# A two-layer decoder trunk on one core: first weights on ScalarE's queue, the norms' vectors in front of x, the first products in another order, and a planner with new durations and a margin for TensorE

## The chip, the core and the metric

One NeuronCore of a Trainium2 chip. The metric is the device time of one launch in microseconds (us), the median of several runs. Engines: PE (TensorE; PEld is its weight load), DVE (VectorE), ACT (ScalarE), POOL (GpSimd), SP (SyncE, which here issues nearly all DMAs).

## What is computed

A trunk of two layers over 256 tokens with 1024 features, in float32; layer 0 mixes by block attention, layer 1 by a three-branch sparse attention, and each is followed by a gated per-layer embedding.

```python
for i in range(2):
    h = rms_norm(x, norm_gain[i])
    x = x + (moba_layer if i == 0 else nsa_layer)(h, ...)
    gate = sigmoid(rms_norm(x, ple_gate_gain[i]) @ ple_w_gate[i])
    x = x + gate * (p[i] @ ple_w_proj[i])
def moba_layer(h):
    q, k, v, z = split(h @ w_in, 4)          # 1024 columns each
    return (attention(rope(norm(q)), rope(norm(k)), v) * silu(z)) @ w_out
```

With 256 tokens and blocks of 256 the first layer is plain causal attention over 16 heads.

## The kernel before

All of x (features on partitions, 8 k-tiles of 128 by 256 tokens) stays on the core; the weights, 59 MB in all, stream through. A product is made from three: every operand is split into a rounded part `hi` and a remainder `lo` (for x: `ah` and `al`), and PE forms hi·ah, hi·al and lo·ah. `hi` and `ah` are made on ACT (some on DVE), `lo` and `al` on DVE: `lo` = raw - hi. A weight tile is two k-tiles of 512 columns (128x1024, 512 KB), with five buffers each for `raw`, `hi` and `lo`. The norm's scale comes in late: products are made from x times its gain, and 1/rms is applied to their results, so PE can start before the norm is known.

The program is recorded, not issued: `Plan.record` notes each operation with what it reads and writes and its cost in ns (`Plan.cost`), `Plan.schedule` simulates the engines in order of time and gives each engine its order, and `Plan.emit` issues it. So every instruction has the one line L366 (`emit`), and whatever changes a cost changes the order on all engines. The choice in `schedule`: for each engine the ready operation with the smallest (earliest start, recorded number), then the engine whose choice starts first.

The start: PE runs 15 products of zeros (`warm`). Meanwhile SP issues x's first k-tile, half of the first weight tile, x's second k-tile, the second weight tile, and so on; ACT's queue issues the norms' vectors (`gain_in`, 16 KB) and the other half of the first weights, loads its function table with a tiny Exp (`early`), and makes `ah`. The first unit `uq0` (512 columns of q) takes one k-tile at a time, k = 0 to 7, into banks of PSUM `mm`; then `norm` sums the squares (`sqacc`) over partitions by PE products with `ones` (written to `tr`), DVE makes `ms` from it, and the unit `uk` (k of the first half of the heads) follows with tiles of 128x1024, which need `lo` from DVE. `tq` and `tk` are DVE products of the rotary tables `cst` with the heads' gains `gmoba`, two SP transfers. Then come v, the attention of 8 heads in pairs (`sm` are its probabilities, transposed by PE into `tr`; `hl`, `qk` the split q and k; `s` the scores), the second half, the gate z, the output product, the embedding, and the second layer in the order of `ORDER`, where `kg`, `pc`, `kcB`, `vcB` belong to its branches.

Of the kernel before, what the change touches and what calls it, by code (L numbers as in the profile page):

```python
# [7 lines left out]
F32 = mybir.dt.float32  # L8
# [11 lines left out]
SWITCH, POW = 150.0, 2300.0  # L20
NRAW, NHI, NLO, NPT, NA = 5, 5, 5, 9, 9
WARM = 15
ORDER = ("vw KE vs VS KT QE0 0A 0S1 0S0 VW 0T0 0S3 0T1 kc 0S2 1A 0T3 0T2 KC 1S0 1T0 q1.0 1S2 W0 q1.1 q1.2 1S3 "
         "0V 1T2 q1.3 W1 1S1 W2 1T3 W3 QE1 2A WE 2S2 0c 2S0 1c 1T1 1V 2T0 0b 2T2 2c 2S1 1b 2B 3A 3c 2T1 2S3 "
         "3S1 2T3 2V 3S0 3T1 3T0 3B 3S3 3S2 3T2 3T3 3V")
# [57 lines left out]
class Plan:  # L83
# [77 lines left out]
    def cost(self, op, views, first):  # L161
        n = first.elems() if isinstance(first, View) else 0
        e, m = op.engine, op.method
        if e == "sync":
            v = first if isinstance(first, View) else op.args[1]
            return v.elems() * 4 * v.ap.ap[0][1]
        if e == "tensor":
            k, c = op.args[1].ap.ap[0][1], op.args[1].ap.ap[1][1]
            op.mode = tuple(128 if x > 64 else 64 if x > 32 else 32 for x in (k, c))
            if m == "transpose":  # L170
                return 109.2
            if op.args[1].ap.dtype == mybir.dt.bfloat16:
                return 2.5 + n / 1.2
            if op.args[1].ap.dtype == F32R:
                return (n + 32) / 2.4 if n > 128 else 110

            return 2 * max(54.6 if op.mode == (128, 64) else 109.2, 2 * n / 2.4 / (2 if op.mode == (128, 64) else 1))
        if e == "gpsimd":
            if op.kwargs.get("op") == OP.pow:
                return POW + 130.0 * n  # L180
            return 100 + 2.3 * n
        psum = any(self.tags[v.tile.tag]["psum"] for v in views)
        rows = first.ap.ap[0][1]
        half = 110 if rows in (60, 64) and (any(v.box()[0] != first.box()[0] for v in views)
                                            or psum and first.ap.dtype == F32R and e == "vector") else 0
        if e == "scalar":
            if m == "dma_start":
                return first.elems() * 4 * first.ap.ap[0][1]
            if first.tile.tag == "early":
                return 1500.0  # L190
            c = (60 if psum else 100) + 0.833 * max(n, op.args[1].elems())
            return half + c + 93 * sum(isinstance(op.kwargs.get(k), View) for k in ("scale", "bias", "accum_out"))
        if m == "tensor_tensor_reduce":
            return 130 + 1.04 * n
        if m == "reciprocal":
            return 65 + 6.9 * n
        if m == "tensor_reduce":
            return 65 + 1.04 * op.args[1].elems()
        two = len([v for v in views if v.elems() > 2 and v is not first]) > 1
        if not psum and not two and m in ("tensor_copy", "tensor_scalar"):  # L200
            return 70 + half + 0.52 * n + 60 * any(isinstance(x, View) and x.elems() == 1 for x in op.args[2:])
        if m == "tensor_tensor" and args_step(op.args[1]) >= 16:
            return 65 + 1.75 * n
        return 65 + half + 1.04 * n + (65 if m == "scalar_tensor_tensor" and isinstance(op.args[2], View) else 0)

    LAT = {"PE": 200.0, "DVE": 140.0, "ACT": 160.0, "POOL": 200.0, "DMA": 100.0}
    START = {"PE": 110.0}

    ISSUE, LAG, RATE = 450.0, 2250.0, ((6000.0, 225.0), (26000.0, 280.0), (1e9, 340.0))
    OWN = {"DVE": 127.0, "POOL": 127.0}  # L210

    def lat(self, a, b):
# [24 lines left out]
    def schedule(self):  # L237
# [43 lines left out]
        while len(order) < n:  # L281
            best = None
            for e, lst in ready.items():
                if not lst:
                    continue
                if e in forced:
                    lst = [forced[e]]
                f = free[e]
                ch = None
                for i in lst:  # L290
                    at = alloc_time(i)
                    if at is None:
# [10 lines left out]
                if ch and (best is None or ch < best[0]):  # L303
                    best = (ch, e)
            if best is None:
                raise RuntimeError("no order")
            (s, i), e = best
            o = ops[i]
            for w in o.ways:
                ready[self.ENGINES[w[0]]].remove(i)  # L310
# [77 lines left out]
def trunk(ctx: ExitStack, tc: tile.TileContext, a, out):  # L388
# [44 lines left out]
    cosc, sinc = cs("cosc")[:60], cs("sinc")[:60]  # L433
    repl = cs("repl")[:60].rearrange("p (g r) -> p g r", g=4)

    neg_half = consts.tile([P, 16], F32, name="neg_half")
    nc.vector.memset(neg_half, -0.5)
    warm = work.tile([P, T], mybir.dt.bfloat16, tag="sm", name="warm", bufs=5)
    nc.vector.memset(warm, 0.0)
    ones = consts.tile([P, 2], F32, name="ones")  # L440
    nc.vector.memset(ones, 1.0)

# [8 lines left out]
    def load(src, n, small=False, queue=None):  # L451
        raw = tmp("raw") if small else wpool.tile([P, 1024], F32, tag="raw", name="raw", bufs=NRAW)
        raw = raw[:, :n]
        (queue or nc.sync).dma_start(raw, src)
        return raw
# [13 lines left out]
    def split_act(src, gain=None):  # L469
        hi = apool.tile([P, T], F32R, tag="ah", name="ah")  # L470
        lo = apool.tile([P, T], F32R, tag="al", name="al")
        if gain is None:
            nc.scalar.activation(hi, src, AF.Copy)
            nc.vector.tensor_tensor(lo, src, hi.bitcast(F32), op=OP.subtract)
        else:
            nc.scalar.activation(hi, src, AF.Copy, scale=gain)
            nc.vector.scalar_tensor_tensor(lo, src, gain, hi.bitcast(F32), op0=OP.mult, op1=OP.subtract)
        return hi, lo

    class Unit:  # L480
# [14 lines left out]
        def mul(self, w, j, k, b, ms=(0, 1), cols=None):  # L495
            (wh, wl), (xh, xl) = w, self.xs[k]
            first, last = k == 0, k == self.nk - 1
            if self.feat:
# [7 lines left out]
            else:  # L506
                c0, c1 = cols or (0, self.n)
                o, s = self.ps[b][:, c0:c1], slice(b * P, b * P + P)
                nc.tensor.matmul(o, xh[:, s], wh[:, j], start=first and c0 == 0, stop=False, skip_group_check=True)
                nc.tensor.matmul(o, xl[:, s], wh[:, j], start=False, stop=False, skip_group_check=True)  # L510
                nc.tensor.matmul(o, xh[:, s], wl[:, j], start=False, stop=last, skip_group_check=True)

        def step(self, g):
            w = self.weights(g)
# [218 lines left out]
    uq0.ps = [bank("mm", 4) for _ in range(2)]  # L733

    since = len(nc.ops)
    second = load(a["moba_in"][0, 0, :, 256:512], 256, True, nc.scalar)
    nc.scalar.activation(consts.tile([P, 16], F32, name="early"), neg_half, AF.Exp)
    nc.together(since)
    for k in range(KT):
        nc.sync.dma_start(xT[:, k], a["x"][:, k])  # L740
        x0.append(split_act(xT[:, k], ng[:, 0, k:k + 1]))
        n = 256 if k == 0 else 512
        for c in range(0, 512, n):
            c0 = 512 * (k % 2) + c
            w = split(a["moba_in"][0, k // 2, :, c0:c0 + n], (1, n), small=k < 4, raw=second if c else None)
            for b in range(2):
                uq0.mul(w, 0, k, b, cols=(c, c + n))
    tab, held_at = [], []

    def moba_half(h):  # L750
# [475 lines left out]
def _arrays(i):  # L1226
    import numpy as np

    def c(v):
        return np.ascontiguousarray(v)  # L1230

    def feat(v):
        return c(v.reshape(KT, P, T).transpose(1, 0, 2))
# [11 lines left out]

    f32 = np.float32
    r = {}
    r["x"] = feat(i["x"][0].T)
    r["p"] = c(i["p"][:, 0].transpose(0, 2, 1).reshape(2, 2, P, T).transpose(2, 0, 1, 3))
    r["gain_in"] = c(np.concatenate([gains(i["norm_gain"]), gains(i["ple_gate_gain"])], 1))  # L1250
# [74 lines left out]
```

## Time and profile before

| what | value |
|---|---|
| three runs | 370.11, 370.19, 370.64 us; median 370.19 us |
| the profiled execution's own time | 370.02 us |
| its span (first to last instruction of the program) | 368.2 us |
| busy share of the span: PE, PEld, DVE, ACT | 98%, 88%, 88%, 73% |
| chain that ended last | PE 77%, DVE 13%, ACT 3%, time of issue 3% |
| granted TensorE clock | full from 3.9 us on |

Matmuls are pipelined, so a busy PE is no sign that it is at its peak: PE's pace is read from the starts of successive products, and its idle time from what the product or its weight load waited for. Time is lost where a product starts late, not where an engine off the chain rests.

### The profile page before, as it was taken

The numbers are of one execution on the slowest core, as the hardware profiler recorded it, in microseconds if no ns is written. First come the engines' busy times: TensorE is split into PE (matmuls) and PEld (weight loads), VectorE is DVE, ScalarE is ACT, GpSimd is POOL, SyncE is SP. The second block draws the span as 40 slices with busy tenths as digits, with TensorE's granted clock in tenths as the row PEclk, the third lists the DMA queues.
The fourth block names the chain that finished last, engine by engine and source line by source line (L and its number), as shares of the span: only waits on it lengthen the run. The fifth ranks groups of instructions, "written<-read, shape, count | busy, mean of one in ns | idle before, by whom it ended". The sixth has DMA issues, their size and how long they took to land.

```text
span 368.2 us, 7137 instructions
## 1 busy us (share of the span) xinstructions
PE 359.8 (98%) x2576; PEld 323.2 (88%) x2576; DVE 325.5 (88%) x803; ACT 268.1 (73%) x583; POOL 33.1 (9%) x21
## 2 busy tenths in 40 slices
PE   7999999999999999999999999999999999999994
PEld 5888888789998999999889998866888998999994
DVE  5999999998799977969979999979989999948864
ACT  5866877777899976737836979587948999937611
POOL 0036002300000000000014000003040000000000
PEclk9999999999999999999999999999999999999998
DMA  7998582546333543551655553085593300545012
GB/s 226 309 371 292 176 264 70 192 154 202 107 141 114 173 163 124 182 179 40 200 165 181 206 185 116 2 287 208 198 323 103 108 9 12 170 164 170 3 36 80
DMA packets 19907, 58.97 MB, mean 160 GB/s; under 512 B 2464, under 2 KB 5152, under 8 KB 19872
## 3 DMA queue, kind: packets, MB, share of 16 engines
q1 hardware_dynamic: 19584, 58.37, 46.7%
q8 instruction: 20, 0.33, 0.3%
q10 hardware_dynamic: 288, 0.15, 0.1%
q14 instruction: 15, 0.12, 0.1%
HBM read 57.46 MB, written 1.05 MB: 159 GB/s over the span
## 4 chain that ended last, share of the span: by engine, by line
PE 77%; DVE 13%; ACT 3%; issue 3%; POOL 1%; DMA 1%; SPq 0%; DVEq 0%; ACTq 0%
PE mm L366 58%; PE tr L366 11%; PE s L366 8%; DVE lo L366 3%; DVE sm L366 3%; DVE tmp L366 2%; DVE q L366 1%; POOL cs L366 1%; DMA tmp<-in_moba_in 1%; DVE big L366 1%; ACT ah L366 1%; ACT sm L366 1%; ACT hl L366 1%; DVE hl L366 1%; ACT qk L366 1%
## 5 line engine op out<-in xcount | busy, mean ns | idle before, releaser
L366 ACT ACTIVATE hi<-raw 128x1024 fp32r<-128x1024 f32 (+2 forms) x100 | 99.4, 1006 | 33.8 <-PE mm L366 17.5
L366 DVE TENSOR_TENSOR lo<-raw,hi 128x1024 fp32r<-128x1024 f32 (+2 forms) x100 | 114.8, 1158 | 5.6 <-ACT hi L366 5.1
L366 PE MATMUL mm<-ah,lo 128*128 128x256 f32 x416 | 118.4, 287 | 0.7 <-DVE lo L366 0.7
L366 PE MATMUL mm<-ah,hi 128*128 128x256 f32 x416 | 118.6, 287 | 0.0
L366 PE MATMUL mm<-al,hi 128*128 128x256 f32 x416 | 118.4, 286 | 0.0
L366 PEld LDWEIGHTS mm<-ah,lo 128*128 128x128 f32 x416 | 79.3, 191 | 1.6 <-DVE lo L366 1.1
L366 PEld LDWEIGHTS mm<-al,hi 128*128 128x128 f32 x416 | 79.7, 192 | 0.4
L366 PEld LDWEIGHTS mm<-ah,hi 128*128 128x128 f32 x416 | 79.4, 191 | 0.3
L366 PE MATMUL mm<-hi,ah 128*128 128x512 f32 (+2 forms) x178 | 66.8, 378 | 0.3 <-DVE hi L366 0.3
L366 PE MATMUL mm<-hi,al 128*128 128x512 f32 (+2 forms) x178 | 66.6, 375 | 0.5 <-DVE al L366 0.5
L366 PE MATMUL mm<-lo,ah 128*128 128x512 f32 (+2 forms) x178 | 66.6, 376 | 0.1
L366 ACT ACTIVATE sm<-sm,nb 128x128 f32<-128x128 f32 (+1 forms) x96 | 42.7, 446 | 8.1 <-DVE nb L366 8.0
L366 PEld LDWEIGHTS mm<-hi,al 128*128 128x128 f32 x178 | 33.6, 189 | 5.9 <-DVE al L366 0.7
L366 PEld LDWEIGHTS mm<-lo,ah 128*128 128x128 f32 x178 | 33.8, 190 | 5.5 <-DVE lo L366 0.4
L366 PEld LDWEIGHTS mm<-hi,ah 128*128 128x128 f32 x178 | 33.3, 188 | 5.6 <-ACT ah L366 0.5
L366 DVE CUSTOM_DVE_ANT_0 sm<-s,cst,nr_q 128x128 f32<-128x128 f32 (+1 forms) x96 | 35.4, 408 | 1.0 <-PE s L366 0.7
L366 PE MATMUL tr<-cst,sm 128*128 128x128 f32 x144 | 24.8, 280 | 0.2 <-DVE sm L366 0.2
L366 ACT ACTIVATE pt<-tr 128x384 f32<-128x384 f32 x48 | 21.6, 481 | 2.0 <-PE tr L366 1.8
L366 POOL TENSOR_TENSOR r_q<-r,neg_half 128x16 f32<-128x16 f32 x5 | 14.8, 2963 | 81.6 <-DVE r L366 81.6
L366 ACT ACTIVATE tmp<-tmp 128x512 f32<-128x512 f32 (+2 forms) x21 | 11.1, 535 | 15.0 <-DVE tmp L366 15.0
L366 POOL TENSOR_TENSOR rstd<-ms,neg_half 128x2 f32<-128x2 f32 x4 | 3.1, 772 | 205.0 <-DVE ms L366 205.0
L366 PEld LDWEIGHTS tr<-cst,sm 128*128 128x128 f32 x144 | 16.9, 141 | 4.7 <-ACT sm L366 1.4
(169 smaller groups left out, 550.3 us busy)
## 6 DMA issues: line engine op xcount, KB each, us to landing
raw<-in_moba_in SPq DMA_DIRECT2D x28, 512.0 KB, 4.5
raw<-in_nsa_in SPq DMA_DIRECT2D x24, 512.0 KB, 4.2
raw<-in_w_out SPq DMA_DIRECT2D x16, 512.0 KB, 3.6
raw<-in_ple_gate SPq DMA_DIRECT2D x16, 512.0 KB, 3.7
raw<-in_w SPq DMA_DIRECT2D x8, 512.0 KB, 4.0
raw<-in_ple_proj SPq DMA_DIRECT2D x4, 512.0 KB, 4.4
raw<-in_nsa_vs SPq DMA_DIRECT2D x4, 304.0 KB, 2.8
xT<-in_x SPq DMA_DIRECT2D x8, 128.0 KB, 4.3
```

What stands on the lines that cost most here:

```text
L366: getattr(getattr(self.nc, o.engine), o.method)(*[real(x) for x in o.args], **{k: real(x) for k, x in o.kwargs.items()})
```

## The change

What it does, in order:

- The norms' vectors are put in front of x's first k-tile, in one transfer of 128x288 by SP; `gain_in` and its transfer go away.
- Both halves of the first weights, and one half of the second k-tile's weights, are issued on ACT's queue; SP issues the other half of the second after x's second k-tile. The second k-tile's raw weights take a buffer of the `raw` pool.
- k-tile 0's twelve products are recorded as hi·ah and hi·al of both halves, then lo·ah of both. Its `ah` may be made on DVE or ACT (`either`); the planner leaves it on ACT.
- `warm` is zeroed before `neg_half`.
- The planner: other durations (below), and for PE an operation's rank is the latest of its start and of its inputs' arrival from other engines plus `MARGIN` = 100 ns, where before it was the start. The rank is only for the choice; the start it simulates is as before.

```diff
@@ Plan.cost
             if op.args[1].ap.dtype == mybir.dt.bfloat16:
-                return 2.5 + n / 1.2
+                return n / 2.4
-                                            or psum and first.ap.dtype == F32R and e == "vector") else 0
+                                            or psum and first.ap.dtype == F32R and m == "activation") else 0
-            c = (60 if psum else 100) + 0.833 * max(n, op.args[1].elems())
+            c = (60 if psum else 110) + 0.833 * max(n, op.args[1].elems())
-        return 65 + half + 1.04 * n + (65 if m == "scalar_tensor_tensor" and isinstance(op.args[2], View) else 0)
+        return 65 + half + 1.055 * n + (65 if m == "scalar_tensor_tensor" and isinstance(op.args[2], View) else 0)
-    ISSUE, LAG, RATE = 450.0, 2250.0, ((6000.0, 225.0), (26000.0, 280.0), (1e9, 340.0))
+    ISSUE, LAG, RATE = 450.0, 2250.0, ((4800.0, 380.0), (7000.0, 250.0), (26000.0, 280.0), (1e9, 340.0))
@@ Plan.schedule
-                    key = (s, i)
+                    late = s
+                    if e == "PE":
+                        late = max([s] + [t + self.lat(o, e) + MARGIN for t, o in came[i] if o and o != "PE"])
+                    key = (late, i, s)
...
-                t = max(s + self.LAG, moved)
+                t = max(s + (self.LAG if s > 3000.0 else 2000.0), moved)
-                finish[i] = free[e] = s + o.cost * (1.8 if e == "PE" and s < 5200.0 else 1.0)
+                finish[i] = free[e] = s + o.cost * (2.0 if e == "PE" and s < 3850.0 else 1.0)
@@ trunk
-    xT = consts.tile([P, KT, T], F32, name="xT")
-    gain_in = consts.tile([P, 4, KT], F32, name="gain_in")
-    nc.scalar.dma_start(gain_in, a["gain_in"])
+    xg = consts.tile([P, 4 * KT + KT * T], F32, name="xg")
+    gain_in = xg[:, :4 * KT].rearrange("p (a k) -> p a k", a=4)
+    xT = xg[:, 4 * KT:].rearrange("p (k t) -> p k t", k=KT)
...
-    second = load(a["moba_in"][0, 0, :, 256:512], 256, True, nc.scalar)
+    early = [load(a["moba_in"][0, 0, :, c:c + 256], 256, True, nc.scalar) for c in (0, 256)]
+    second = wpool.tile([P, 1024], F32, tag="raw", name="raw", bufs=NRAW)[:, :512]
+    nc.scalar.dma_start(second[:, 256:512], a["moba_in"][0, 0, :, 768:1024])
     nc.scalar.activation(consts.tile([P, 16], F32, name="early"), neg_half, AF.Exp)
-    nc.together(since)
+    for o, i in zip(nc.ops[since + 1:], range(since, len(nc.ops))):
+        o.after.append(i)
     for k in range(KT):
-        nc.sync.dma_start(xT[:, k], a["x"][:, k])
-        x0.append(split_act(xT[:, k], ng[:, 0, k:k + 1]))
...
+        lo, hi = 4 * KT + k * T if k else 0, 4 * KT + k * T + T
+        nc.sync.dma_start(xg[:, lo:hi], a["x"][:, lo:hi])
+        if k == 1:
+            nc.sync.dma_start(second[:, :256], a["moba_in"][0, 0, :, 512:768])
+        x0.append(split_act(xT[:, k], ng[:, 0, k:k + 1], k == 0))
+        if k == 0:
+            ws = [split(None, (1, 256), True, raw) for raw in early]
+            for part in ((0, 1), (2,)):
+                for c, w in enumerate(ws):
+                    for b in range(2):
+                        uq0.mul(w, 0, 0, b, cols=(256 * c, 256 * c + 256), parts=part)
+            continue
+        c0 = 512 * (k % 2)
+        w = split(a["moba_in"][0, k // 2, :, c0:c0 + 512], (1, 512), small=k < 4, raw=second if k == 1 else None)
+        for b in range(2):
+            uq0.mul(w, 0, k, b)
```

How the order moves, at three places. First, PE at the end of k-tile 0 and in k-tile 1 (rows of before, then of the change; `mm_78` and `mm_79`, after the change `mm_77` and `mm_78`, are the banks of the two token halves):

```order
41 L366 MATMUL mm_79<-hi_107,al_97 128x256
42 L366 MATMUL mm_79<-lo_112,ah_88 128x256
43 L366 MATMUL mm_78<-hi_108,ah_89 128x512
44 L366 MATMUL mm_78<-hi_108,al_98 128x512
45 L366 MATMUL mm_78<-lo_113,ah_89 128x512
46 L366 MATMUL mm_79<-hi_108,ah_89 128x512
47 L366 MATMUL mm_79<-hi_108,al_98 128x512
48 L366 MATMUL mm_79<-lo_113,ah_89 128x512
```
```order
41 L371 MATMUL mm_77<-lo_116,ah_92 128x256
42 L371 MATMUL mm_78<-lo_116,ah_92 128x256
43 L371 MATMUL mm_77<-hi_112,ah_93 128x512
44 L371 MATMUL mm_77<-hi_112,al_102 128x512
45 L371 MATMUL mm_78<-hi_112,ah_93 128x512
46 L371 MATMUL mm_78<-hi_112,al_102 128x512
47 L371 MATMUL mm_77<-lo_117,ah_93 128x512
48 L371 MATMUL mm_78<-lo_117,ah_93 128x512
```

The two products with `lo` now come last in a k-tile, for both halves, and so through k-tile 7.

Second, DVE at the end of `uq0` (before, then the change; `lo` of 128x1024 are the first two tiles of `uk`):

```order
28 L366 TENSOR_TENSOR sqacc_77<-sqacc_77,tmp_85 128x256
29 L366 TENSOR_TENSOR lo_115<-raw_120,hi_110 128x1024
30 L366 TENSOR_SCALAR ms_124<-tr_76 128x2
31 L366 TENSOR_SCALAR e_0_128<-ms_124 128x2 x2
32 L366 TENSOR_TENSOR lo_111<-raw_116,hi_106 128x1024
33 L366 TENSOR_TENSOR tq_0_133<-cst_65,gmoba_66 128x128 x2
```
```order
27 L371 TENSOR_TENSOR sqacc_76<-sqacc_76,tmp_83 128x256
28 L371 TENSOR_SCALAR ms_123<-tr_75 128x2
29 L371 TENSOR_TENSOR lo_119<-raw_86,hi_114 128x1024
30 L371 TENSOR_SCALAR e_0_127<-ms_123 128x2 x2
31 L371 TENSOR_TENSOR tq_0_132<-cst_64,gmoba_65 128x128
32 L371 TENSOR_TENSOR lo_115<-raw_87,hi_110 128x1024
33 L371 TENSOR_TENSOR tq_0_132<-cst_64,gmoba_65 128x128
```

`ms`, which waits for PE's products with `ones`, has moved ahead of the first tile's `lo`, and one `tq`, which waits for the transfer of `gmoba`, ahead of the second's.

Third, PE at the first pair of heads in the attention (before, then the change):

```order
236 L366 MATMUL mm_80<-hi_106,ah_95 128x512
237 L366 MATMUL mm_80<-hi_106,al_104 128x512
238 L366 MATMUL tr_75<-cst_65,sm_70 128x128
239 L366 MATMUL mm_80<-lo_111,ah_95 128x512
240 L366 MATMUL tr_75<-cst_65,sm_70 128x128 x2
241 L366 MATMUL tr_76<-cst_65,sm_71 128x128
242 L366 MATMUL mm_81<-hi_106,ah_95 128x512
243 L366 MATMUL tr_76<-cst_65,sm_71 128x128 x2
```
```order
236 L371 MATMUL mm_79<-hi_110,ah_99 128x512
237 L371 MATMUL mm_79<-hi_110,al_108 128x512
238 L371 MATMUL mm_79<-lo_115,ah_99 128x512
239 L371 MATMUL mm_80<-hi_110,ah_99 128x512
240 L371 MATMUL mm_80<-hi_110,al_108 128x512
241 L371 MATMUL mm_80<-lo_115,ah_99 128x512
242 L371 MATMUL tr_74<-cst_64,sm_68 128x128 x3
243 L371 MATMUL tr_75<-cst_64,sm_69 128x128
```

The transposes of the probabilities now stand four products further back, and three of them together.

## Rows read from the trace of the kernel before

**Rows 1.** The page's first lines: span, busy time and share of two engines.
```profile
span 368.2 us, 7137 instructions
PE 359.8 (98%) x2576; PEld 323.2 (88%) x2576; DVE 325.5 (88%) x803; ACT 268.1 (73%) x583; POOL 33.1 (9%) x21
```
**Rows 2.** Timeline of PE, 4 to 9 us: start, length, operation, idle before it.
```profile
4.52 0.71 PE L366 MATMUL mm<-hi,ah 128*128 128x256 f32 x4 [0.29 <-DVE hi L366]
5.73 0.39 PE L366 MATMUL mm<-hi,al 128*128 128x256 f32 x1 [0.50 <-DVE al L366]
...
7.76 0.51 PE L366 MATMUL mm<-lo,ah 128*128 128x512 f32 x1
8.10 0.40 PE L366 MATMUL mm<-hi,ah 128*128 128x512 f32 x1
...
8.81 0.40 PE L366 MATMUL mm<-hi,ah 128*128 128x512 f32 x1
```
**Rows 3.** Timeline of SP, ACT and DVE in the first 9 us.
```profile
1.17 0.45 ACTq L366 DMA_DIRECT2D tmp<-in_moba_in  x1
2.10 0.43 SPq L366 DMA_DIRECT2D tmp<-in_moba_in  x1
2.95 0.22 ACT L366 ACTIVATE early<-neg_half 128x16 f32<-128x16 f32 x1
3.46 0.51 ACT L366 ACTIVATE ah<-xT,gain_in 128x256 fp32r<-128x256 f32 x1 [0.30 <-DMA gain_in<-in_gain_in]
5.06 0.61 ACT L366 ACTIVATE sqacc<-xT 128x512 f32<-128x512 f32 x1
6.28 0.43 DVE L366 CAST hi<-tmp 128x512 fp32r<-128x512 f32 x1 [0.60 <-DMA tmp<-in_moba_in]
7.57 0.63 ACT L366 ACTIVATE hi<-tmp 128x512 fp32r<-128x512 f32 x1 [0.19 <-DMA tmp<-in_moba_in]
```
**Rows 4.** Timeline of PE, DVE and SP around the end of uq0.
```profile
12.39 0.43 SPq L366 DMA_DIRECT2D gmoba<-in_head_gain  x1
17.00 0.50 PE L366 MATMUL tr<-ones,sqacc 128*128 128x2 f32 x4
17.54 0.16 DVE L366 TENSOR_SCALAR ms<-tr 128x2 f32<-128x2 f32 x1 [0.28 <-PE tr L366]
18.36 0.62 PE L366 MATMUL mm<-lo,ah 128*128 128x512 f32 x2
18.81 1.23 DVE L366 TENSOR_TENSOR lo<-raw,hi 128x1024 fp32r<-128x1024 f32 x1 [0.82 <-ACT hi L366]
19.95 0.49 DVE L366 TENSOR_TENSOR tq<-cst,gmoba 128x128 f32<-128x128 f32 x2
20.62 0.39 PE L366 MATMUL mm<-lo,ah 128*128 128x512 f32 x1
```
**Rows 5.** The tile gmoba: its one transfer, from issue to landing.
```profile
DMA to landing us min/median/max: 6.8/6.8/6.8
```
**Rows 6.** Busy time in stretches: length, PE, PEld, DVE, ACT, POOL, PEclk, DMA share, GB/s.
```profile
12.00:16.00 4.00, 4.00 (x19) 3.32 (x18) 4.00 (x9) 3.52 (x8) 0.00 (x0) 1.00 1.00 329
60.00:70.00 10.00, 10.00 (x59) 7.74 (x58) 10.00 (x22) 7.25 (x16) 0.40 (x1) 1.00 0.53 169
```
**Rows 7.** Waits of PE's weight loads, 40 to 140 us: total, times, longest.
```profile
PEld tr L366 <- DVE sm L366: 1.4, 5, 0.4
```
**Rows 8.** Waits of PE's weight loads, 200 to 330 us: the four largest.
```profile
PEld tr L366 <- ACT sm L366: 1.7, 4, 0.6
...
PEld mm L366 <- DVE lo L366: 1.1, 2, 0.5
PEld s L366 <- DVE nb L366: 0.7, 3, 0.4
PEld tr L366 <- ACT pt L366: 0.6, 2, 0.4
```
**Rows 9.** Groups by form: the copies that build qk, on DVE and on ACT.
```profile
L366 DVE CAST qk<-hl 64x256 fp32r<-64x256 f32 x5 | 1.4, 288 | 3.2 <-ACT hl L366 3.1
L366 ACT ACTIVATE qk<-hl 64x256 fp32r<-64x256 f32 x27 | 11.2, 415 | 0.7
```

More of the change, by code (lines that the diff above doesn't have):

```diff
@@ L22 @@
 WARM = 15
+MARGIN = 100.0
 ORDER = ("vw KE vs VS KT QE0 0A 0S1 0S0 VW 0T0 0S3 0T1 kc 0S2 1A 0T3 0T2 KC 1S0 1T0 q1.0 1S2 W0 q1.1 q1.2 1S3 "
@@ L299, in schedule @@
                         t + self.lat(o, e) if o else t for t, o in came[i]])
-                    key = (s, i)
+                    late = s
+                    if e == "PE":
+                        late = max([s] + [t + self.lat(o, e) + MARGIN for t, o in came[i] if o and o != "PE"])
+                    key = (late, i, s)
                     if ch is None or key < ch:
                         ch = key
-                if ch and (best is None or ch < best[0]):
+                if ch and (best is None or (ch[2], ch[1]) < (best[0][2], best[0][1])):
                     best = (ch, e)
@@ L306, in schedule @@
                 raise RuntimeError("no order")
-            (s, i), e = best
+            (_, i, s), e = best
             o = ops[i]
@@ L434, in trunk @@
     repl = cs("repl")[:60].rearrange("p (g r) -> p g r", g=4)
+    warm = work.tile([P, T], mybir.dt.bfloat16, tag="sm", name="warm", bufs=5)
+    nc.vector.memset(warm, 0.0)
     neg_half = consts.tile([P, 16], F32, name="neg_half")
     nc.vector.memset(neg_half, -0.5)
-    warm = work.tile([P, T], mybir.dt.bfloat16, tag="sm", name="warm", bufs=5)
-    nc.vector.memset(warm, 0.0)
     ones = consts.tile([P, 2], F32, name="ones")
@@ L467, in split, with split_act @@
         return (hi.rearrange("p (a b) -> p a b", a=shape[0]), lo.rearrange("p (a b) -> p a b", a=shape[0]))
-    def split_act(src, gain=None):
+    def split_act(src, gain=None, either=False):
         hi = apool.tile([P, T], F32R, tag="ah", name="ah")
@@ L475, in split_act @@
         else:
-            nc.scalar.activation(hi, src, AF.Copy, scale=gain)
+            if either:
+                nc.copy(hi, src, gain)
+            else:
+                nc.scalar.activation(hi, src, AF.Copy, scale=gain)
             nc.vector.scalar_tensor_tensor(lo, src, gain, hi.bitcast(F32), op0=OP.mult, op1=OP.subtract)
@@ L493, in weights, with mul @@
             return split(self.src[g], (self.kg, self.n))
-        def mul(self, w, j, k, b, ms=(0, 1), cols=None):
+        def mul(self, w, j, k, b, ms=(0, 1), cols=None, parts=(0, 1, 2)):
             (wh, wl), (xh, xl) = w, self.xs[k]
@@ L508, in mul @@
                 o, s = self.ps[b][:, c0:c1], slice(b * P, b * P + P)
-                nc.tensor.matmul(o, xh[:, s], wh[:, j], start=first and c0 == 0, stop=False, skip_group_check=True)
-                nc.tensor.matmul(o, xl[:, s], wh[:, j], start=False, stop=False, skip_group_check=True)
-                nc.tensor.matmul(o, xh[:, s], wl[:, j], start=False, stop=last, skip_group_check=True)
+                for i in parts:
+                    x, y = ((xh, wh), (xl, wh), (xh, wl))[i]
+                    nc.tensor.matmul(o, x[:, s], y[:, j], start=first and c0 == i == 0, stop=last and i == 2,
+                                     skip_group_check=True)
         def step(self, g):
@@ L735, in trunk @@
     since = len(nc.ops)
-    second = load(a["moba_in"][0, 0, :, 256:512], 256, True, nc.scalar)
+    early = [load(a["moba_in"][0, 0, :, c:c + 256], 256, True, nc.scalar) for c in (0, 256)]
+    second = wpool.tile([P, 1024], F32, tag="raw", name="raw", bufs=NRAW)[:, :512]
+    nc.scalar.dma_start(second[:, 256:512], a["moba_in"][0, 0, :, 768:1024])
     nc.scalar.activation(consts.tile([P, 16], F32, name="early"), neg_half, AF.Exp)
-    nc.together(since)
+    for o, i in zip(nc.ops[since + 1:], range(since, len(nc.ops))):
+        o.after.append(i)
     for k in range(KT):
-        nc.sync.dma_start(xT[:, k], a["x"][:, k])
-        x0.append(split_act(xT[:, k], ng[:, 0, k:k + 1]))
[L742 to L747, printed above, removed]
+        lo, hi = 4 * KT + k * T if k else 0, 4 * KT + k * T + T
[14 more added lines that the diff above has]
+            uq0.mul(w, 0, k, b)
     tab, held_at = [], []
@@ L1247, in _arrays @@
     r = {}
-    r["x"] = feat(i["x"][0].T)
+    r["x"] = c(np.concatenate([v.reshape(P, -1) for v in (gains(i["norm_gain"]), gains(i["ple_gate_gain"]),
+                                                          feat(i["x"][0].T))], 1))
     r["p"] = c(i["p"][:, 0].transpose(0, 2, 1).reshape(2, 2, P, T).transpose(2, 0, 1, 3))
-    r["gain_in"] = c(np.concatenate([gains(i["norm_gain"]), gains(i["ple_gate_gain"])], 1))
     r["moba_in"] = units(i["moba_w_in"][0], [s(512 * u) for u in range(8)])
```

## The prediction

> **What bounds the kernel now.** I read the page's first lines, then PE's own timeline at the start, then who PE's weight loads waited for in the rest. PE is busy for 359.8 of 368.2 us [rows 1], so the time is PE's number of products times its pace, plus the places where a product starts late. The pace stands in rows 2: the first product of k-tile 1's last three starts at 8.10 and k-tile 2 begins at 8.81, so a 512-column product takes 0.71 / 3 = 0.24 us. The change neither adds nor removes a product. So it can only win or lose at late starts, and these are small. At the start PE waits 0.29 us for `hi`, 0.50 for `al`, and its first lo·ah of k-tile 1 comes only at 7.76, 0.6 after the product ahead of it (the listing's 7.76 against 8.10 shows the pace taken up again) [rows 2]. Between 40 and 140 us five waits for probabilities make 1.4 us [rows 7]. Between 200 and 330 us the four largest kinds make 1.7 + 1.1 + 0.7 + 0.6 = 4.1 us in 4 + 2 + 3 + 2 = 11 waits [rows 8]. Together these are 5.5 us in 16 waits, 0.34 us each: all that a better order can win there.
>
> DVE is the engine next to the bound. It is full in 12 to 16 us (4.00 of 4) and again in 60 to 70 us (10.00 of 10), beside a PE as full [rows 6]. What is put on DVE there delays something.
>
> **Baseline.** The profiled execution took 370.02 us, 0.17 below the median of 370.19. I make the sum against 370.02 and add 0.17 at the end. I take 0.2% (0.74 us) as what a measurement here can tell from no change, so "same" is 369.45 to 370.93.
>
> **Part 1, the first weights.** Before, k-tile 1's weights were issued by SP at 2.10 as 256 KB, and DVE's `hi` waited for them until 6.28, 4.2 us after the issue [rows 3]. Now they go as two halves, in the third place of ACT's queue and of SP's. Issues take about 0.45 us each and ACT's first began at 1.17 before, behind the vectors', so the third of either is issued at about 1.6 to 2.1. At the same 4.2 us they would land at 5.8 to 6.3. The best bound is the first half itself: issued at 1.17, with its product, `hi` included, at 4.52 [rows 2, 3], so about 3.0 us for the transfer, and 1.6 + 3.0 = 4.6. Between 4.6 and 6.3 I take 5.4: nearer to the middle, since x's first tiles and the first weights are still in flight ahead of them.
>
> What follows is set by ACT. The third issue pushes the table load (`early`, 2.95 + 0.22) and the first `ah` back: 2.95 + 0.45 + 0.22 = 3.62 against 3.46 [rows 3]. That costs at most 0.16; I take nothing, since PE's first product waited for DVE's `hi`, not for `ah` [rows 2], and `ah` no longer has the vectors' transfer of its own to wait 0.30 for [rows 3]. Then ACT makes the second `ah` and squares (5.06 + 0.61 = 5.67 [rows 3]) and k-tile 1's `hi`, which has moved from DVE (0.43) to ACT (0.63, as k-tile 2's at 7.57): 5.67 + 0.63 = 6.3. Six products of 0.24 are 1.4, so k-tile 2 begins at 7.7 to 7.8 instead of 8.81: a gain of 1.0, with bounds 0.4 (landing at 6.3, below) and 1.2. The wait for `lo` at 7.76 should go too, because both lo·ah now stand last and `lo` has two products more, 0.5 us. DVE, though full, passes the shift on: its work from here is the same and starts earlier. The vectors' one transfer with x, `warm` ahead of `neg_half` and `either` (the planner leaves `ah` on ACT) I cost at nothing: they lie beside the 15 warming products, and if that cover went, the 0.16 above is the price.
>
> **Part 2, the end of uq0.** This takes most of it back. The products with `ones` began at 17.00 and would now begin at 16.0. DVE's `ms` waits for them; it started 0.54 later and took 0.16 [rows 4]. It now stands ahead of the `lo` of uk's first tile, which takes 1.23. So that `lo` is ready at 16.0 + 0.54 + 0.16 + 1.23 = 17.93, while PE wanted it 18.36 - 17.00 = 1.36 after the `ones` products, at 17.36. Loss 0.6; of the 1.0, 0.4 is left. Behind `ms`, the next thing queued is one `tq`, ahead of the second tile's `lo`. It waits for `gmoba`, issued at 12.39 [rows 4] and 6.8 under way [rows 5]: 19.2. Its issue may come up to 0.4 earlier, so I take 19.0. Then 0.25 (half of `tq`'s 0.49) and 1.23 for `lo` give 20.48. PE reached this `lo`'s product at 20.62 before [rows 4] and would reach it at 20.22 now. So 0.26 more goes, and the first 20 us give **-0.14 us** in all. The bounds: -0.4 if `gmoba` lands by 18.7, +0.1 if it lands at 19.2.
>
> **Part 3, the planner.** The new durations and the margin are to let PE pass over a product whose inputs are only just due. The order shows it at the first pair of heads: the transposes of probabilities stand four products, some 0.9 us, further back, where the longest wait for them was 0.4 [rows 7]. No row of before can show what a new order costs, so I bound it: the most is all of the 5.5 us of rows 7 and 8; the least is none, or a loss. Products put ahead of a late one cost nothing when they are themselves ready, but whoever waits for the late one gets it later. The value I take is the margin itself: 100 ns in each of 16 waits is 1.6 us, less one new wait of the mean size, 0.3: **-1.3 us**.
>
> The same planner gives DVE more to do in the attention: six of the copies that build `qk` go from ACT to DVE (5 become 11, 27 become 21). At 0.288 us each that is 1.7 us of DVE [rows 9], and ACT loses 6 x 0.415 = 2.5. I take zero: full as DVE is, it held PE back by only 1.4 us in 100 there [rows 7], so it works ahead of PE. Without that lead the price is the whole 1.7.
>
> **Sum.** 370.02 - 0.14 - 1.3 = 368.6; with 0.17, **368.8 us**.
>
> **A row and a rule on Part 1.** The trace has k-tile 1's weights 4.2 us under way from SP [rows 3], and the first half about 3.0 from ACT; two queues could be what made the second faster. The Trainium skill ("DMA: Bandwidth & Descriptors", section "Issuing engines are not separate DMA queues") says that transfers run on the same 16 engines and interleave whichever engine starts them, so that issuing from several saves only the issuing time. No row here decides between the two; the rule's case is the second rival.
>
> **The rivals.**
>
> *The planner's part buys nothing.* Each wait that is healed comes back at another place, since DVE is full [rows 6] and PE's inputs still come from it. For it: 5.5 us in 300 is little, and 16 waits of 0.34 look like the remainder of any order. Against it: the waits for `sm` are of one kind, and these transposes are moved. Time 370.02 - 0.14 + 0.17 = 370.1. Chance 0.23.
>
> *The first weights come no earlier.* The bytes ahead of k-tile 1's weights are the same as before, and they land at 6.3 again. ACT's `hi` then ends at 6.9, k-tile 2 begins at 8.4, and the gain is 0.4; `ms` takes 0.6, and PE reaches the second `lo` at 20.62 - 0.4 + 0.6 = 20.8, after it is ready: 0.2 slower. 370.02 + 0.2 - 1.3 + 0.17 = 369.1. Chance 0.15.
>
> *Slower: DVE becomes the bound in the first attention.* Six copies more, 1.7 us, fall where DVE is 10.00 of 10 busy [rows 6]. It decides if the lead of `lo` over PE there is shorter than these 1.7; then PE waits for `lo` or `qk`, and the margin's win is halved, as its reserve is DVE's too: 370.02 - 0.14 + 1.7 - 0.65 + 0.17 = 371.1. Against it: rows 7. Chance 0.17.
>
> *The margin heals more.* Three fifths of 5.5 us go, 3.3: 370.02 - 0.14 - 3.3 + 0.17 = 366.8. Chance 0.08.
>
> That the change does not do what it says holds for `either` alone, and that is in the sum at nothing.
>
> **How the numbers follow.** The forecast has 0.37. Faster: 0.37 + 0.15 + 0.08, less 0.03 for the edge of the second rival's 369.1 towards 369.45, is 0.57. Same: 0.23 + 0.03 = 0.26. Slower: 0.17. The range goes from 366.6, just past the last rival, to 371.3, just past the slower one; it leaves out a half of each and a few hundredths beyond all cases, 0.17 in all. The likeliest case's own range is 368.2 to 369.4.
>
> **What the new profile would show.** Right: PE begins k-tile 2 at 7.7 to 7.8 (8.4 if the weights come no earlier); a wait of 0.6 for `lo` after the `ones` products, which begin at about 16.0; DVE's `tq` waiting for `gmoba`, and PE at the second tile's lo·ah at about 20.5; few or no waits for `sm` in 40 to 140 us, and fewer than 4.1 us of waits in 200 to 330. Wrong: those sums as large as before under other names (the first rival), or waits of PE for `lo` or `qk` between 60 and 140 us that make 1 us or more (the slower one); or a start whose gain survives to 20.6, because `lo` is ready though `ms` stands ahead of it.

## The result, and the profile after

| kernel | median | range | runs |
|---|---|---|---|
| before, beside it | 370.20 us | 369.96 to 370.64 | 11 |
| changed | 368.14 us | 367.68 to 369.83 | 11 |

The ratio is 0.9950, 95% interval 0.9938 to 0.9962: 2.06 us faster. The forecast was 368.8, 1.4 us faster. The profiled execution of the change took 368.94 us, 0.8 above its median. So I also use the profile of a second execution of the same kernel (367.71 us), called the second profile below.

To see where time goes I took from each trace when PE had started the same amount of work, each product counted at the usual pace of its shape. This is worked out, not a view. The numbers are us behind (+) or ahead (-) of the kernel before, at times of the kernel before:

| | 8 us | 18 us | 24 us | 80 us | 140 us | 200 us | 270 us | 330 us |
|---|---|---|---|---|---|---|---|---|
| change, profiled | -0.43 | +0.36 | +1.45 | +1.38 | -0.69 | -0.51 | -2.00 | -1.13 |
| change, second profile | -0.61 | -0.44 | +0.27 | +0.18 | -1.90 | -1.72 | -3.20 | -2.33 |

At 80 and 140 us, where the two orders mix different products, the numbers move by some 0.2 us with the way of counting. Both have the same shape: a start that ends up behind, then 2.6 us gained from 24 us to the end, most of it in the first attention (80 to 140) and in the sparse one (200 to 270).

The page's first lines, against [rows 1]; PE is busy 0.8 us less in a span 1.1 shorter:

```profile
span 367.1 us, 7127 instructions
PE 359.0 (98%) x2576; PEld 322.3 (88%) x2576; DVE 325.6 (89%) x806; ACT 269.0 (73%) x580; POOL 35.6 (10%) x21
```

PE's timeline of the change, profiled execution, against [rows 2, 4] (start, length, operation, idle before it and releaser):

```profile
4.69 1.38 PE L371 MATMUL mm<-hi,ah 128*128 128x256 f32 x4 [0.26 <-ACT ah L371]
...
6.85 0.40 PE L371 MATMUL mm<-hi,ah 128*128 128x512 f32 x1
...
8.24 0.39 PE L371 MATMUL mm<-hi,ah 128*128 128x512 f32 x1
...
11.66 0.50 PE L371 MATMUL mm<-hi,ah 128*128 128x512 f32 x1 [0.42 <-ACT hi L371]
...
17.36 0.50 PE L371 MATMUL tr<-ones,sqacc 128*128 128x2 f32 x4
...
18.50 0.39 PE L371 MATMUL mm<-hi,al 128*128 128x512 f32 x1
19.26 0.73 PE L371 MATMUL mm<-lo,ah 128*128 128x512 f32 x2 [0.38 <-DVE lo L371]
...
21.89 0.50 PE L371 MATMUL mm<-lo,ah 128*128 128x512 f32 x1
```

K-tile 1's first product, before and in the second profile:

```profile
6.85 0.47 PE L366 MATMUL mm<-hi,ah 128*128 128x512 f32 x1
```
```profile
6.67 0.40 PE L371 MATMUL mm<-hi,ah 128*128 128x512 f32 x1
```

K-tile 1 begins at 6.85, as before, and k-tile 2 at 8.24 instead of 8.81 (6.67 and 8.06 in the second profile). But then PE waits near 11.66 for `hi`, at 19.26 for `lo` and, without a mark, at 21.89, 0.46 after the product before it where 0.23 is the pace. SP, ACT and DVE tell why, in the same execution, against [rows 3, 4]:

```profile
2.59 0.43 SPq L371 DMA_DIRECT2D tmp<-in_moba_in  x1
4.25 0.33 SPq L371 DMA_DIRECT2D xg<-in_x  x1
...
13.21 0.42 SPq L371 DMA_DIRECT2D gmoba<-in_head_gain  x1
```
```profile
4.09 1.03 ACT L371 ACTIVATE ah<-xg 128x256 fp32r<-128x256 f32 x2 [0.45 <-DMA xg<-in_x]
...
5.94 0.63 ACT L371 ACTIVATE hi<-raw 128x512 fp32r<-128x512 f32 x1 [0.29 <-DMA raw<-in_moba_in]
...
10.97 0.63 ACT L371 ACTIVATE hi<-raw 128x512 fp32r<-128x512 f32 x1 [1.06 <-DMA raw<-in_moba_in]
```
```profile
17.90 0.16 DVE L371 TENSOR_SCALAR ms<-tr 128x2 f32<-128x2 f32 x1 [0.97 <-PE tr L371]
17.98 1.23 DVE L371 TENSOR_TENSOR lo<-raw,hi 128x1024 fp32r<-128x1024 f32 x1
...
20.41 0.29 DVE L371 TENSOR_TENSOR tq<-cst,gmoba 128x128 f32<-128x128 f32 x1 [1.05 <-DMA gmoba<-in_head_gain]
20.62 1.22 DVE L371 TENSOR_TENSOR lo<-raw,hi 128x1024 fp32r<-128x1024 f32 x1
```

SP pauses for 1.2 us between its fifth transfer (2.59) and its sixth (4.25, the ninth with ACT's three), where its steps are else 0.47. Its waits in the first 24 us name the first weights' landing:

```profile
SPq L371 <- DMA tmp<-in_moba_in: 1.7, 2, 1.2
```

The trace's operands show eight semaphores for the landings, used in turn: the ninth transfer waits until the first has landed. Before, the first was the vectors' 16 KB, and the ninth was issued at 3.53; now it is half of the first weights.

In this execution the transfers behind it come later too: `gmoba` is issued at 13.21, not 12.39. The pause alone does not do that: the second profile has it as well (from 2.58 to 4.16) and issues `gmoba` when the kernel before did:

```profile
12.38 0.42 SPq L371 DMA_DIRECT2D gmoba<-in_head_gain  x1
```

In the profiled execution DVE stands still for 0.97 us for `ms` and 1.05 for `tq`, with the `lo` that PE wants behind each.

The waits of PE's weight loads, 40 to 140 us and then 200 to 330 us, against [rows 7, 8]:

```profile
PEld tr L371 <- issue: 0.9, 4, 0.4
PEld mm L371 <- issue: 0.2, 1, 0.2
```
```profile
PEld tr L371 <- ACT sm L371: 1.0, 3, 0.4
...
PEld s L371 <- DVE nb L371: 0.6, 2, 0.4
PEld tr L371 <- DVE tmp L371: 0.6, 3, 0.2
PEld tr L371 <- DVE c L371: 0.6, 1, 0.6
PEld mm L371 <- DVE lo L371: 0.5, 1, 0.5
```

The five waits for probabilities (1.4 us) are gone whole. The kinds that made 4.1 us in 11 waits now make 2.5 in 7, `pt`'s 0.4 included; some came back under other names (`tmp`, `c`). With every kind counted but `issue`, the waits fall from 1.7 us to none in the first stretch and from 5.5 to 4.7 in the second: 2.5 us, close to the 2.6 by PE's position.

### The profile page after: what moved, and what is told of

It is laid out like the page before. It is cut to its first block, busy times and chain, and to the rows that moved or that the text cites. A ratio compares the mean times of both kernels' runs of the same rounds, so it can differ in the third digit from the quotient of the medians.

```text
span 367.1 us, 7127 instructions
## 1 busy us (share of the span) xinstructions
PE 359.0 (98%) x2576; PEld 322.3 (88%) x2576; DVE 325.6 (89%) x806; ACT 269.0 (73%) x580; POOL 35.6 (10%) x21
## 3 DMA queue, kind: packets, MB, share of 16 engines
HBM read 57.46 MB, written 1.05 MB: 159 GB/s over the span
## 4 chain that ended last, share of the span: by engine, by line
PE 77%; DVE 13%; DMA 4%; issue 2%; POOL 1%; SPq 1%; ACT 0%; DVEq 0%; ACTq 0%
PE mm L371 59%; PE tr L371 10%; PE s L371 8%; DVE lo L371 3%; DVE tmp L371 2%; DVE sm L371 2%; DMA gmoba<-in_head_gain 2%; DMA raw<-in_moba_in 1%; POOL cs L371 1%; DVE q L371 1%; DMA tmp<-in_moba_in 1%; DVE pc L371 1%; DVE big L371 1%; DVE vcB L371 1%; SPq L371 1%
## 5 line engine op out<-in xcount | busy, mean ns | idle before, releaser
L371 PE MATMUL mm<-lo,ah 128*128 128x512 f32 (+2 forms) x178 | 65.1, 376 | 0.4 <-DVE lo L371 0.4
L371 POOL TENSOR_TENSOR rstd<-ms,neg_half 128x2 f32<-128x2 f32 x4 | 4.9, 1234 | 203.3 <-DVE ms L371 203.3
```

Source lines behind the costliest of these rows:

```text
L371: getattr(getattr(self.nc, o.engine), o.method)(*[real(x) for x in o.args], **{k: real(x) for k, x in o.kwargs.items()})
```

## The experiments

All times are medians. The runs were made in three groups, and ratios are to the kernel before in the same group, which took 370.23, 370.62 and 370.23 us. The change run again beside the last group gave 367.86 us, ratio 0.9937 (0.9925 to 0.9949).

### One part of the change alone

**start_only**: the changed start under the old planner.

```diff
-                return n / 2.4
+                return 2.5 + n / 1.2
...
-                        late = max([s] + [t + self.lat(o, e) + MARGIN for t, o in came[i] if o and o != "PE"])
-                    key = (late, i, s)
+                    key = (s, i)
```

> The changed start (transfers, order of k-tile 0 and of the products with lo) under the old planner: old durations, no margin. Theory A, from the trace of the change (PE stands 1.4 us behind the kernel before at 24 us, after waits for late weights at 11.66, for lo at 19.26 and 21.89): the start itself costs time, because SP's ninth transfer has to wait for the first one to land (issued at 4.25 instead of 3.06) and all later weights come later. Then 0.6 to 1.4 us slower than before, 370.8 to 371.6, with SP waiting for the first weights' landing and PE waiting near 11 us for hi. Rival B: the start is worth the 0.14 us that was predicted, and what was lost by 24 us is the new planner's doing (ms and tq put ahead of lo). Then 369.8 to 370.3 and no wait of PE between 8 and 24 us.

Measured: 370.40 us, 1.0009 (0.9993 to 1.0025). No difference. PE stood 0.50 behind at 24 us; at 18 it was 0.22 ahead, and a wait for `lo` behind `ms` came between (0.54 above the pace). Theory A's size was wrong, and B's "no wait" too: the old planner also puts `ms` ahead of `lo` with this start. PE loses nothing near 11 us.

**plan_only**: the new planner with the old start, transfers included.

```diff
+MARGIN = 100.0
...
-    ISSUE, LAG, RATE = 450.0, 2250.0, ((6000.0, 225.0), (26000.0, 280.0), (1e9, 340.0))
+    ISSUE, LAG, RATE = 450.0, 2250.0, ((4800.0, 380.0), (7000.0, 250.0), (26000.0, 280.0), (1e9, 340.0))
```

> The new planner (durations and margin) with the old start. Theory A: the planner gives all of the gain and more: 2.5 to 3 us from 40 us on, nothing lost ahead of it, so 367.2 to 367.9, 0.3 to 0.9 below the change. Rival B: it brings the loss at the end of uq0 along: 368.3 to 369.

Measured: 373.14 us, 1.0072 (1.0055 to 1.0090): 2.9 us slower, against both theories. Its timelines of PE and of DVE:

```profile
4.41 0.71 PE L371 MATMUL mm<-hi,ah 128*128 128x256 f32 x4
7.73 0.58 PE L371 MATMUL mm<-hi,al 128*128 128x256 f32 x1 [2.61 <-DVE al L371]
```
```profile
4.38 0.75 DVE L371 TENSOR_TENSOR lo<-tmp,hi 128x256 fp32r<-128x256 f32 x2
6.12 0.43 DVE L371 CAST hi<-tmp 128x512 fp32r<-128x512 f32 x1 [0.99 <-DMA tmp<-in_moba_in]
6.58 0.69 DVE L371 TENSOR_TENSOR lo<-tmp,hi 128x512 fp32r<-128x512 f32 x1
7.19 1.27 DVE L371 SCALAR_TENSOR_TENSOR al<-xT,gain_in,ah 128x256 fp32r<-128x256 f32 x3
```

K-tile 1's `hi` and `lo` now stand ahead of k-tile 0's `al` on DVE, as if the planner took the weights for earlier than they were. DVE stood at the `hi` until 6.12, and PE for 2.61 us. Behind that rest the granted clock was at its lower level for a while (columns as in [rows 6]):

```profile
8.00:9.00 1.00, 1.00 (x6) 1.00 (x7) 1.00 (x4) 0.93 (x3) 0.00 (x0) 0.50 0.99 250
```

PE was 2.0 us behind when it took up hi·al (7.73 against 5.73 in [rows 2]) and 2.70 at 24 us. What came after is not settled: from 24 to 270 us this kernel gained 1.59, the change 3.45, and then it lost that again, with the clock at 0.50 once more from 281 to 283.

**plan_nodma**: as plan_only, but with the old numbers for transfers (`RATE`, `LAG`) and for PE's slow start.

```diff
-    ISSUE, LAG, RATE = 450.0, 2250.0, ((4800.0, 380.0), (7000.0, 250.0), (26000.0, 280.0), (1e9, 340.0))
+    ISSUE, LAG, RATE = 450.0, 2250.0, ((6000.0, 225.0), (26000.0, 280.0), (1e9, 340.0))
```

> The old start, with the margin and the new durations of PE, DVE and ACT, but the planner's old numbers for transfers and for PE's slow start. Theory A: the planner's new numbers for transfers fit only the new start, and with the old start they alone made it 2.9 us slower (al put behind a hi that waits for a transfer, PE waiting 2.6 us at 7.73); without them the old start keeps its 370.2 pace up to 24 us and the planner's gain of 2.5 us after it is had: 367.4 to 368.2. Rival B: the margin and durations have no sure gain, each new order is a draw: 369 to 371.

Measured: 367.84 us, 0.9924 (0.9908 to 0.9940), as theory A said. PE is 0.40 behind at 24 us and gains 2.55 after that. The planner's numbers for transfers and for PE's slow start are all that divides it from plan_only's 373.14. So the old start with the new durations and the margin is as fast as the whole change.

**margin_zero**: the change with `MARGIN = 0.0`. **margin_only**: the kernel before with the margin, old durations and old start.

```diff
-MARGIN = 100.0
+MARGIN = 0.0
```

> The change with MARGIN = 0 (new durations stay). If the margin is what heals PE's small waits: up to 40 us as the change, then PE waits for sm between 40 and 140 us come back (1 to 1.5 us) and some in 200 to 330, so 369.3 to 370.2. If the durations do it: within 0.4 us of the change, 367.8 to 368.5.

```diff
+MARGIN = 100.0
...
-                    key = (s, i)
...
+                        late = max([s] + [t + self.lat(o, e) + MARGIN for t, o in came[i] if o and o != "PE"])
+                    key = (late, i, s)
```

> The kernel before with the margin of 100 ns alone: old durations, old start. If the margin is what heals the small waits: no waits for sm between 40 and 140 us, 1.3 to 2.5 us faster than before, 367.7 to 368.9. If the durations do it: 369.8 to 370.5.

Measured: margin_zero 369.14 us, 0.9972 (0.9961 to 0.9984); margin_only 370.36 us, 1.0003 (0.9991 to 1.0015). Neither gives the change's gain. After 24 us margin_zero gains 1.36 of the 2.6. Margin_only stands 0.90 behind at 24 us, after late products from 10 us on, and 0.21 ahead at 270. So from 24 to 270 us, by one profile each, the margin alone gains 1.1, the durations without it 1.5 (+2.12 to +0.63), and both together 3.45. The waits that remain between 40 and 140 us, of margin_zero and of margin_only:

```profile
PEld tr L371 <- DVE sm L371: 0.6, 3, 0.3
PEld tr L371 <- issue: 0.5, 3, 0.2
PEld tr L371 <- ACT pt L371: 0.4, 1, 0.4
```
```profile
PEld tr L371 <- DVE sm L371: 1.4, 4, 0.5
```

With the old durations the margin leaves the waits for `sm` as long as they were (1.4 us); with the new ones and no margin 0.6 is left; with both, none. My expectation of margin_only was wrong. My reading, which no run tests, is that 100 ns do not help where the planner's time for the input is off by more.

The profiled execution of margin_only was 1.55 us above its median, and its windows show one reason, a lower clock (columns as in [rows 6]):

```profile
279.00:280.00 1.00, 1.00 (x4) 0.58 (x4) 0.97 (x5) 0.95 (x4) 0.00 (x0) 0.50 0.02 8
...
281.00:282.00 1.00, 1.00 (x6) 1.00 (x6) 0.94 (x4) 0.49 (x1) 0.00 (x0) 0.50 0.00 0
```

### Single places, with every other order kept

These edit the change's own order after it is planned, so that nothing else moves; only the last, margin_200, is planned anew.

**lo_first**: on DVE the two `lo` in front of `ms` and of `tq`, as before.

```diff
+    ahead(los[0], next(i for i in dve if tag(nc.ops[i]) == "ms"))
+    ahead(los[1], next(i for i in dve if tag(nc.ops[i]) == "tq1"))
```

> The change with its own order, but on DVE the lo of uk's first tile ahead of ms and that of the second ahead of tq, as they stood before; no other engine's order is touched. If these two are what PE waits for at 19.26 (0.4 to 0.5 us) and 21.89 (0.2): both waits gone and PE 0.7 us earlier from 22 us to the end, 367.4 to 367.6 (the change 368.14). Rival, the wait is only handed on (ms late makes q late, tq late makes the scores late): within 0.2 us of the change.

Measured: 367.63 us, 0.9914 (0.9896 to 0.9932). PE is 0.23 ahead at 24 us, and both waits are gone. PE of lo_first, against 19.26 above:

```profile
17.90 0.39 PE L371 MATMUL mm<-hi,al 128*128 128x512 f32 x1
18.13 0.62 PE L371 MATMUL mm<-lo,ah 128*128 128x512 f32 x2
```

Nothing is handed on: its gain after 24 us is 2.60, as in the change.

**one_transfer**: k-tile 1's weights as one transfer of 256 KB, SP's third.

```diff
+    order.remove(act_half)
+    nc.ops[sp_half].args = (second, a["moba_in"][0, 0, :, 512:1024])
```

> The change with its own order on PE, DVE, ACT and POOL, but k-tile 1's weights in one transfer of 256 KB from SP instead of two halves. Theory A, the number of transfers: with one fewer in flight SP's ninth becomes k-tile 3's weights; its wait for the first landing shrinks from 1.2 us (issued at 4.25 instead of 3.06) to about 0.2, the weights of k-tile 4 land about 0.8 earlier than at 10.87, no wait of PE at 11.66 (0.42), gmoba earlier than 20.31: 0.5 to 0.7 us faster than the change, 367.4 to 367.7. Rival B, the rate of the transfers sets the landings and not the issue: same landings after 8 us, within 0.2 us of the change, or 0.4 slower since k-tile 1's weights come at 6.3 instead of 5.9.

Measured: 368.03 us, 0.9929 (0.9912 to 0.9946). SP's pause is shorter (0.7 us) and falls one transfer later. Between 10 and 12 us PE still loses 0.46, where it loses 0.80 in the change's profiled execution and 0.15 in its second profile, so the edit shows no gain there; the times are equal within the intervals. Rival B's loss did not come either: ACT's `hi` starts at 5.94, as in the change.

**transfers_old**: the change's order, with the first transfers as before (vectors apart and first, half of the first weights on SP, k-tile 1's weights in one). **transfers_old_lo**: the same with lo_first's edit.

```diff
...
+    nc.ops[act_first].args = (xg[:, :4 * KT], a["x"][:, :4 * KT])
+    nc.ops[sp_x0].args = (xg[:, 4 * KT:4 * KT + T], a["x"][:, 4 * KT:4 * KT + T])
+    nc.ops[act_half].engine, nc.ops[act_half].args = "sync", (w0, a["moba_in"][0, 0, :, 0:256])
+    nc.ops[sp_half].args = (second, a["moba_in"][0, 0, :, 512:1024])
...
```

> The change with its own order on PE, DVE and POOL, but the first transfers as before: the vectors apart and first on ACT's queue, x's first k-tile alone, one half of the first weights on SP, k-tile 1's weights in one transfer. Theory A: the new transfers are what the start loses. x's first tile lands at 3.2 instead of 4.1, the first product starts at 4.4 instead of 4.7, SP's ninth transfer is not held (3.5 instead of 4.25), no wait near 11 us; the waits for lo at 19 and 22 stay: 0.3 to 0.6 us faster than the change. Rival B: k-tile 1's weights come at 6.3 instead of 5.9, ACT's hi at 6.9, and this takes all of it back: within 0.2 us of the change, or slower.

> As the run before, and the two lo ahead of ms and tq: both mended. Theory A: the two add up, 0.7 us for the lo and 0.3 to 0.6 for the transfers: 0.9900 to 0.9915 of before, the fastest kernel of the study. Rival B: as lo_first without the old transfers, 0.9914, or worse.

> The change itself once more, beside the three below. The runs so far put its usual start 0.6 us behind the kernel before at 24 us and its gain after that at 2.6, so 0.9940 to 0.9950 of before; the profiled execution had 1.45 at 24 us, of which the wait at 11.66 is a part that need not come again.

Measured: transfers_old 367.88 us, 0.9942 (0.9930 to 0.9954); transfers_old_lo 367.32 us, 0.9926 (0.9913 to 0.9939); the change again 0.9937. Theory A fell: the old transfers give neither gain nor loss. PE's timeline of transfers_old:

```profile
4.67 1.15 PE L371 MATMUL mm<-hi,ah 128*128 128x256 f32 x3 [0.23 <-DVE hi L371]
...
7.13 0.50 PE L371 MATMUL mm<-hi,ah 128*128 128x512 f32 x1 [0.22 <-ACT hi L371]
```

The first product is no earlier (4.67, and 4.61 in the change's second profile), because it now waits for `hi` where it waited for `ah`. K-tile 1's `hi` starts at 6.44, and PE waits for it, which is what the new transfers mend. By 18 us little of that is left: transfers_old is 0.23 ahead of the kernel before, the change's second profile 0.44, one_transfer 0.09. What the new transfers lose on the way is not settled. SP's pause is a candidate, but start_only has it too (2.58 to 4.46) and loses nothing between 8 and 18 us. The `lo` edit alone is worth 0.56 us (367.88 to 367.32), as its wait said. The lowest median of the study is transfers_old_lo's 367.32; by ratio lo_first (0.9914) is its equal within the intervals.

**warm18**: three more products of zeros.

```diff
...
+    order[order.index(last):order.index(last)] = [last] * 3
```

> The change with three more products of zeros ahead of the first real one (18 instead of 15), nothing else moved. In the profiles so far the first products run at half pace (0.21 us for 256 columns, as the zeros do) until about 3.9 us in two executions, 5.9 in three and 10.2 in one, and the spread of the times is 1.5 to 2 us. Theory A: PE's rest between the last zero (4.2) and the first product (4.69) is what leaves the clock low in some executions; with PE kept busy until 4.65 the spread shrinks and the median falls by 0.2 to 0.5 us, 367.6 to 367.9. Rival B: the rise comes when it comes, whatever stands there: the same median and spread as the change; if the zeros run over the first product's start, 0.1 slower.

Measured: 368.01 us, 0.9926 (0.9910 to 0.9943): the same as the change again within the intervals. In its profile the trace's record of the granted clock begins, at the upper level, at 4.73, ahead of the first product at 4.93; in the change's two profiles at 5.94 and 4.17 (and in start_only, which my expectation counts with the 5.9, at 4.76). One profile can't show that the zeros did it, nor can five runs settle the spread. Neither theory is shown.

**margin_200**: the change with twice the margin.

```diff
-MARGIN = 100.0
+MARGIN = 200.0
```

> The change with a margin of 200 ns instead of 100; the order differs from the change's only after 40 us. If 100 ns already cover what the planner's durations miss (no wait for sm left from 40 to 140 us): within 0.4 us of the change, and PE's waits between 200 and 330 us as large as there. If the margin's size is what counts: 0.5 to 1 us faster, with fewer waits from 200 to 330 us.

Measured: 370.65 us, 1.0022 (1.0009 to 1.0036): 2.8 us slower than the change. Both expectations fell. At 140 us it stands where the change's second profile does (-1.88 against -1.90). Then PE, and ACT beside it:

```profile
139.45 1.16 PE L371 MATMUL tr<-cst,sm 128*128 128x128 f32 x6
141.12 1.52 PE L371 MATMUL tr<-pt,v 128*64 128x256 f32 x16 [0.51 <-ACT pt L371]
144.24 0.98 PE L371 MATMUL mm<-ah,hi 128*128 128x256 f32 x6 [1.60 <-ACT ah L371]
```
```profile
140.58 0.87 ACT L371 ACTIVATE pt<-tr 128x384 f32<-128x384 f32 x2
142.69 0.60 ACT L371 ACTIVATE big<-tr 128x512 f32<-128x512 f32 x1 [1.24 <-PE tr L371]
143.78 0.75 ACT L371 ACTIVATE ah<-big 128x256 fp32r<-128x256 f32 x2 [0.49 <-DVE big L371]
```

The larger margin let PE take every other ready product ahead of the last pair's transposes. Then nothing was left to cover the chain from the last transposes over `pt` and `big` to the output product's `ah`: 0.51 + 1.60 us of waits, and some 3 us by PE's position between 140 and 200. In the change PE goes on at 139.73, right behind the sixteen products of `pt` and `v`, with products that it had kept. That the margin should have an upper end was not in my theories.

## Why the prediction was right, and where it was not

The time (368.14) lies in the range, and the sign was right. The sum got there by luck in part: its two terms were off in opposite directions.

- **First weights, forecast 5.4 and k-tile 2 at 7.7 to 7.8.** ACT's `hi` waited for them until 5.94 in the profiled execution and started at 5.59, without a marked wait, in the second profile. K-tile 2 began at 8.24 and 8.06: 0.57 and 0.75 gained, not 1.0. What failed is the step that lets k-tile 1 begin when its `hi` ends, at 6.3. That `hi` ended at 6.57 and 6.21, but k-tile 1 began at 6.85 and 6.67, right behind k-tile 0's own products, which my sum had left out; before, it began at 6.85 too. So 0.57 of the gain is that k-tile 1's six products, with no late one among them, take 1.39 us instead of 1.96. The price that I took as nothing did come: the first product started at 4.69 and 4.61 instead of 4.52. The late first `ah` (4.09 and 4.00 instead of 3.46) is not all of it, since transfers_old has that `ah` at 3.14 and its first product at 4.67, behind `hi`. The rival's 6.3 did not come about.
- **`ms` ahead of `lo`, forecast 0.6.** PE's lo·ah came 0.76 after the product ahead of it instead of 0.23: 0.53 lost. lo_first and transfers_old_lo show it by removal.
- **`tq` ahead of the second `lo`, forecast ready at 20.48.** In the profiled execution `gmoba` was issued 0.8 later, not up to 0.4 earlier, and `lo` ended at 21.84. In the second profile it was issued at 12.38 and `lo` ended at 20.50, as forecast, and PE, behind for the other reasons, did not wait. I had not seen SP's pause: I took its third issue to be early and asked nothing of its later ones. What made `gmoba` late in the one execution, with the same pause in both, stays open.
- **The first 20 us, forecast -0.14 in all**: by 24 us +0.27 in the second profile, +1.45 in the profiled execution. start_only and plan_nodma show that the start as a whole buys nothing.
- **The planner, forecast -1.3.** This is the term that was mis-sized: 2.6 us from 24 us on, in both profiles of the change and in every other kernel with both parts, except plan_only and margin_200. The step "100 ns in each of 16 waits" failed. A margin does not shave its own length off each wait; it decides which product goes first, and a transpose that goes four products back escapes its whole wait. And the durations did about half by themselves (margin_zero: 1.36), for which I had given no term of their own. The upper bound, all of 5.5 us, held.
- **The `qk` copies at zero.** Right: between 40 and 140 us no wait of PE names DVE.
- **The rivals.** "The planner buys nothing" fell with plan_nodma, "slower by DVE" with those waits. "The margin heals more" (3.3 us) was nearer in its term than my forecast was; its time, 366.8, was too low because the start gave nothing.

More rows bear on the rule weighed there. K-tile 1's `hi` started at 5.94 with the weights in one transfer on SP's queue (one_transfer), and at 5.94 and 5.59 with two halves on two queues. With the one transfer issued 0.45 later it started at 6.28 (before) and 6.44 (transfers_old). The Trainium skill ("DMA: Bandwidth & Descriptors", section "Issuing engines are not separate DMA queues") says that a second issuing engine saves only the time of issue; these rows agree.

## What to carry to other kernels

A planner's margin and its durations each won a part behind the start (1.1 and 1.5 us by 270 us), and more together (3.45) than the two alone; the margin alone left the whole program's time where it was. A planner's numbers for transfers belong to the transfers they were fitted to: plan_only, with one set and the other start, took 373.14 us, plan_nodma 367.84. A margin has an upper end too, where it eats the work that should cover the next hand-over. And when an order changes everywhere, compare PE's position stretch by stretch: here a total of -2.06 hid a start that had turned out slower.

## What was not expected of the hardware

PE's pace in the first microseconds differs between executions. The zeros run 0.21 us apart for 256 columns, and later products of that size 0.12. In margin_zero's profiled execution, 1.7 us above its own median, the half pace lasted to 10.2:

```profile
5.95 1.05 PE L371 MATMUL mm<-hi,al 128*128 128x256 f32 x4
...
8.08 0.63 PE L371 MATMUL mm<-hi,al 128*128 128x512 f32 x1
8.51 0.63 PE L371 MATMUL mm<-hi,ah 128*128 128x512 f32 x1
...
10.47 0.39 PE L371 MATMUL mm<-hi,al 128*128 128x512 f32 x1
10.70 0.40 PE L371 MATMUL mm<-hi,ah 128*128 128x512 f32 x1
```

The first two starts of 512 columns are 0.43 us apart, the last two 0.23: the lower and the upper of the two levels, 1.2 and 2.4 GHz. The profile's column of the granted clock shows 1.00 all through this, but only because nothing is recorded there yet: the trace's first record of the clock, at the upper level, begins at 10.25, where the pace rises. It begins at 3.86 in the kernel before, and at 5.94 and 4.17 in the change's two profiles; in the first of these the products up to there ran at the zeros' pace, which may be a part of its worse start. So early on the pace of the products has to be read, and not the column. What decides when the clock rises was not settled: PE had done the same zeros in each case. Nor was the fall in margin_only at 279 us, which plan_only and margin_200 show at about the same place of the program and the change's two profiles don't.
